# Softmax attention heads in pairs, in two row tiles and two column tiles of TensorE

## The chip, the cores and the metric

The kernel runs on one core of a Trainium2 chip. The metric is the device time of one execution in microseconds (us). The kernel before has a median of 1285.93 us over 3 runs (1284.1 to 1291.37).

## What is computed

A decoder trunk of four residual layers over 256 tokens of width 1024, batch 1. Layer 0 and layer 3 mix tokens with sliding-window attention (SWA: 16 query heads, 4 key/value heads, head width 64, window 128, rotary, a learned sink logit per head). Layer 1 is gated linear attention (GLA). Layer 2 is forgetting attention (FoX: 16 heads, no rotary, a cumulated log forget gate added to the scores). Every mixer is followed by a dense SwiGLU network (FFN). The two softmax mixers are what matters here:

```python
# swa_mixer, per block n of 128 queries, over this block's and the previous block's keys
scores = einsum('bnqkgd,bnskd->bnkgqs', qb, kk) * hd ** -0.5      # masked to the band
probs = softmax(concatenate([scores, sink_col], -1))[..., :-1]
out = einsum('bnkgqs,bnskd->bnqkgd', probs, vv) ; return out @ w_o
# fox_mixer, per block i of 128 queries, over all keys up to t1
s = einsum('bhqd,bhkd->bhqk', q, k) * hd ** -0.5 + lc[t0:t1] - lc[:t1]   # causal
o = einsum('bhqk,bhkd->bhqd', softmax(s), v) ; return o @ w_o
```

## The kernel before

Activations lie feature by token (8 tiles of 128 features by 256 tokens). Weights are float32; each piece of a weight is split by ACT (`wh`, L195) and DVE (`wl`, L197) into a high and a low part, and a product with weights is three matmuls (`mm3`, L260 to L262). Conditioning vectors (`ada`) are made on DVE (L217) or POOL (L212). A `Stream` holds the weights in order of use with five raw buffers; the SP queue issues the next load when a buffer is free.

The order of the work is written out by a Python generator. The projections call `tick()` after every two k steps; each tick emits a share of the pending weight pieces and, if a background generator runs, `bg_rate` steps of it. The background generator of the softmax layers is `attn_heads` (L529): it emits a part of the attention and yields. It is started after the first group of queries and runs beside the three other groups' projections (8 ticks each) and then beside the first half of the output projection (`out_proj`, 16 ticks), where `need_k(k)` forces as many steps as the k-th 128 features of the output need, and `bg_drain` ends it. The rates are `BG_SWA` (start rate, steps already due, rate in the output projection; first layer 0, then layer 3) and `FOX_RATE`.

`attn_heads` goes head by head in a pipeline of depth three. In iteration n it emits, up to its first `yield`: the scores of head n (L544: 128 queries by 128 keys; L545: 128 queries by 256 keys; float32, which the chip runs as two matmuls each) into one PSUM bank of tag `s` (2 buffers); the products with v of head n-2 (L551, L552) into 64 of the 128 rows of the bank `o` (1 buffer); for head n-1 the reciprocal of the row sums (DVE, L556) and the scaling of the probabilities (ACT L557 for block 0, DVE L558 for block 1); then for head n the masked minimum (DVE, L572, two instructions) and the exponentials with row sums (ACT, L577, two instructions). Up to its second `yield`: three transposes of head n-1's probabilities (PE, L585) into a bank `t` (2 buffers) and their copy to `pt` (ACT, L596); for every second head the split of `o` into `oh`, `ol` (L493, L494) that the output projection reads. That is 19 iterations of 2 steps, 38 steps.

In SWA the q and k of an even head lie in partitions 0 to 63 and those of an odd head in partitions 64 to 127, so that the matmuls L544 and L545 contract over 64 rows of the array. In FoX they contract over 66 rows from partition 0 (64 of the head and 2 for the gate). In both, a head's product with v has 64 columns of weights, and odd and even heads write to different halves of the bank `o`. The queries of SWA are transposed four heads at a time (`swa_qT`, L644), called by `pre` two heads ahead.

```python
sc = self.ps("s")
nc.tensor.matmul(sc[:, :P], q[:, :P], k[:, :P], start=True, stop=True)          # L544
nc.tensor.matmul(sc[:, P:3 * P], q[:, P:], k, start=True, stop=True)            # L545
...
nc.tensor.matmul(o[rows, :S], v[0], pt[:, :S], start=True, stop=False)          # L551
nc.tensor.matmul(o[rows, P:S], v[1], pt[:, S:], start=False, stop=True)         # L552
```

The framework that builds the program may set an engine's instructions in another order than they are written, within their dependencies; the trace shows the order in which they ran.

Of the kernel before, what the change touches and what calls it, by code (L numbers as in the profile page):

```python
# [13 lines left out]
AF = mybir.ActivationFunctionType  # L14
ALU = mybir.AluOpType
PSUM = bass.MemoryType.PSUM

P = 128
D = 1024
KT = D // P  # L20
S = 256
NB = S // P
DEPTH = 4
HD = 64
# [4 lines left out]
BIG = 1e30  # L29
# [24 lines left out]
RAW = 5  # L54
MIX_POOL = ((), (), (), ())
ORDER0 = "wshshshhwswwwgwwgggSwHSwHSSHHw"
BG_SWA = ((1.05, -6.5, 3.9), (0.544, 2.0, 1.367))
ROPE_ADD = (('gpsimd', 'gpsimd'), ('vector', 'vector'))
EARLY = 2
POOL_ADA = {(0, 0): (0, 1, 2, 4, 5), (0, 1): (7,), (0, 2): (1, 3, 4), (0, 3): (0, 1, 2, 4, 5), (0, 4): (1, 3, 4, 7)}  # L60
# [6 lines left out]
MIX_SPAN = (3, -2)  # L67
GLA_ORDER = ('z', 'r1', 'q0', 'k0', 'b', 'k1', 'q1', 'r2', 'v1', 'r3', 'v2', 'v3')
GLA_RATE = (0.585, 2.55)
FOX_RATE = (0.556, -7.0, 0.586, 0.885)  # L70
STAT = (1, 1, 1)
PSBUFS = {"mm": 3, "s": 2, "t": 2, "o": 1}

# [70 lines left out]
class Builder:  # L144
# [384 lines left out]
    def attn_heads(self, pool, heads, mask, oh, ol):  # L529


        nc = self.nc
        n_heads = len(heads)
        sms, prs, pts, rds, os_ = {}, {}, {}, {}, {}
        blocks = ((0, P, 0, P), (P, 3 * P, 129, 385))
        heads[0]["pre"]()
        for n in range(n_heads + 3):
            if n < n_heads:
                hd = heads[n]
                while not hd["ready"]():  # L540
                    yield
                q, k = hd["q"](), hd["k"]()
                sc = self.ps("s")
                nc.tensor.matmul(sc[:, :P], q[:, :P], k[:, :P], start=True, stop=True)  # L544
                nc.tensor.matmul(sc[:, P:3 * P], q[:, P:], k, start=True, stop=True)  # L545
            j = n - 2
            if 0 <= j < n_heads:
                o = os_[j // 2] = self.ps("o") if j % 2 == 0 else os_[j // 2]
                pt, v = pts.pop(j), heads[j]["v"]()
                rows = slice((j % 2) * HD, (j % 2 + 1) * HD)  # L550
                nc.tensor.matmul(o[rows, :S], v[0], pt[:, :S], start=True, stop=False)  # L551
                nc.tensor.matmul(o[rows, P:S], v[1], pt[:, S:], start=False, stop=True)  # L552
            j = n - 1
            if 0 <= j < n_heads:
                pr, rd, dn = prs[j], *rds.pop(j)
                nc.vector.reciprocal(rd, dn)  # L556
                nc.scalar.activation(pr[:, :P], pr[:, :P], AF.Copy, scale=rd[:, 0:1])  # L557
                nc.vector.tensor_scalar(out=pr[:, 129:385], in0=pr[:, 129:385],  # L558
                                        scalar1=rd[:, 1:2], scalar2=None, op0=ALU.mult)
            if n < n_heads:  # L560
                sm = self.t(pool, [P, 386], "sm", bufs=2)
                pr = prs[n] = self.t(pool, [P, 386], "pr", bufs=3)
                nm = self.t(self.small, [P, 2], "nm", bufs=3)
                dn = self.t(self.small, [P, 2], "dn", bufs=3)
                rds[n] = (self.t(self.small, [P, 2], "rd", bufs=3), dn)
                ns, e = hd["sink"], 0
                if ns is not None:
                    e = 1
                    nc.gpsimd.tensor_copy(sm[:, P:P + 1], ns)
                    nc.gpsimd.tensor_copy(sm[:, 385:386], ns)  # L570
                for b, (so, s1, po, p1) in enumerate(blocks):
                    nc.vector.tensor_tensor_reduce(  # L572
                        out=sm[:, po:p1], in0=sc[:, so:s1], in1=mask[:, so:s1], scale=1.0,
                        scalar=BIG if ns is None else ns, op0=ALU.add, op1=ALU.min,
                        accum_out=nm[:, b:b + 1])
                for b, (so, s1, po, p1) in enumerate(blocks):
                    nc.scalar.activation(pr[:, po:p1 + e], sm[:, po:p1 + e], AF.Exp, scale=-1.0,  # L577
                                         bias=nm[:, b:b + 1], accum_out=dn[:, b:b + 1])
            yield
            j = n - 1  # L580
            if 0 <= j < n_heads:
                pr = prs.pop(j)
                tp = self.ps("t")
                for i, po in enumerate((0, 129, 257)):
                    nc.tensor.transpose(tp[:, i * P:(i + 1) * P], pr[:, po:po + P], self.c("ident"))  # L585
            if n + 2 < n_heads:
                while not heads[n + 2]["pre"]():
                    yield
            if n >= 3 and n % 2:
                j = (n - 3) // 2  # L590
                self.split_hl(os_.pop(j)[:, :S], oh[:, j], ol[:, j])
                self.done_k = j + 1
            j = n - 1
            if 0 <= j < n_heads:
                pts[j] = self.t(pool, [P, 3 * P], "pt", bufs=2)
                nc.scalar.copy(pts[j], tp[:, :3 * P])  # L596
            yield


# [56 lines left out]
    def swa_heads(self, layer, pool, q_of, kT, v, oh, ol):  # L656
        nc = self.nc
        j = 0 if layer == 0 else 1
        nsink = self.t(pool, [P, 16], "nsink", bufs=1)
        nc.vector.tensor_scalar(out=nsink, in0=self.c("sinks")[:, 16 * j:16 * j + 16], scalar1=-1.0,  # L660
                                scalar2=None, op0=ALU.mult)
        qTs = {}

        def head(h):
            g, i = divmod(h, 4)
            rows = slice((i % 2) * HD, (i % 2 + 1) * HD)

            def pre():
                q = q_of(g)
                if i == 0 and q is not None:  # L670
                    qTs[g] = self.swa_qT(pool, q)
                return q is not None
            return {
                "pre": pre, "ready": lambda: True,
                "q": lambda: qTs[g][rows, i // 2],
                "k": lambda: kT[0][rows, g],
                "v": lambda: [v[:, b, g * HD:(g + 1) * HD] for b in range(NB)],
                "sink": nsink[:, h:h + 1],
            }
        return self.attn_heads(pool, [head(h) for h in range(16)], self.c("swamask"), oh, ol)  # L680
# [37 lines left out]
    def swa(self, layer, oh, ol, pool):  # L718
# [21 lines left out]
        for g in range(4):  # L740
            parts = self.proj_tok(self.st.get(f"i{layer}_{2 + g}"), hs)
            qr[g] = self.swa_q(pool, parts)
            if g == 0:
                self.bg_start(gen, *BG_SWA[layer > 0][:2])
        self.bg_rate = BG_SWA[layer > 0][2]

# [20 lines left out]
    def fox(self, layer, oh, ol, pool):  # L767
# [12 lines left out]
        for g in range(4):  # L780
            if g == 3:
                self.bg_rate = FOX_RATE[2]
            grp[g] = t = [self.t(pool, [66, 4, S], "qA", bufs=2), self.t(pool, [66, 4, S], "kA", bufs=2)]
# [39 lines left out]
            if g == 0:  # L823
                self.bg_start(gen, *FOX_RATE[:2])
        self.bg_rate = FOX_RATE[3]

# [534 lines left out]
```

## Time and profile before

| what | value |
|---|---|
| median of 3 runs | 1285.93 us |
| the profiled execution's own time | 1287.15 us |
| its span, first to last instruction | 1285.4 us |
| granted TensorE clock, mean | 0.993 |
| PE busy | 1223.3 us, 95% of the span |
| DVE busy | 1029.2 us, 80% |
| ACT busy | 719.4 us, 56% |
| attention in layer 0, layer 2, layer 3 | about 73 to 135 us, 698 to 782 us, 1012 to 1075 us |

PE is TensorE's matmuls, DVE VectorE, ACT ScalarE, POOL GpSimd. A matmul's duration holds its way through the array, so consecutive matmuls overlap in the table; what a matmul costs is read from the start of one to the start of the next. Busy shares are means over stages with different limits; a stage is read from its own stretch.

### The profile page before, as it was taken

To read this page: it belongs to the slowest core of one execution; us is meant where nothing else is said; L and a number is where in the kernel's file an instruction comes from. 1 tells how busy PE (TensorE), PEld (TensorE's weight loads), DVE (VectorE), ACT (ScalarE), POOL (GpSimd) and SP (SyncE) were. 2 spreads that over 40 slices of the span, in tenths; PEclk is the share of its full clock that TensorE was granted. 3 is DMA by queue.
4 is the path that set the end of the run, shared out by engine and by line. 5 is a ranking of instruction groups with operands and counts; after the bars stand their busy time and mean duration, and the time that the engine had idled before them with its cause. 6 is when DMAs were issued, how large, how long until landed. Compare 5 with 4: busy or idle time off the path is not lost.

```text
span 1285.4 us, 19492 instructions
## 1 busy us (share of the span) xinstructions
PE 1223.3 (95%) x7284; PEld 1061.3 (83%) x7284; DVE 1029.2 (80%) x1839; ACT 719.4 (56%) x1323; POOL 200.5 (16%) x211
## 2 busy tenths in 40 slices
PE   3698999999999999999999999999999999999997
PEld 2676888888898998888899889888889878888886
DVE  5999998878779889888877657988787977766553
ACT  4567764444576665444448766644445667644442
POOL 5468110001105321000120101100011012000011
PEclk9999999999999999999999999999999999999999
DMA  8665779977744436997875443799777434665450
GB/s 328 256 231 196 267 290 358 340 262 266 264 161 167 165 132 231 352 340 279 271 280 210 157 170 109 275 357 336 273 266 257 168 128 139 222 214 202 161 176 33
DMA packets 44673, 298.50 MB, mean 232 GB/s; under 512 B 5169, under 2 KB 5329, under 8 KB 14242
## 3 DMA queue, kind: packets, MB, share of 16 engines
q1 hardware_dynamic: 43778, 295.53, 63.7%
q8 instruction: 57, 0.93, 0.3%
q10 hardware_dynamic: 432, 1.20, 0.2%
q0 software_dynamic: 368, 0.53, 0.1%
q14 instruction: 38, 0.31, 0.1%
HBM read 296.15 MB, written 1.05 MB: 231 GB/s over the span
## 4 chain that ended last, share of the span: by engine, by line
PE 83%; DVE 9%; ACT 3%; issue 2%; DMA 2%; POOL 1%; DVEq 0%; SPq 0%; POOLq 0%; ACTq 0%
PE mm L1100 13%; PE mm L260 12%; PE mm L261 11%; PE mm L262 11%; PE mm L1102 7%; PE s L260 6%; PE s L261 6%; PE s L262 6%; DVE raw L217 2%; DVE wl L197 2%; PE o L551 2%; PE t L1071 1%; PE s L545 1%; DMA raw<-in_ada 1%; PE t L585 1%
## 5 line engine op out<-in xcount | busy, mean ns | idle before, releaser
L197 DVE TENSOR_TENSOR wl<-raw,wh 128x1024 fp32r<-128x1024 f32 (+2 forms) x408 | 454.6, 1147 | 85.5 <-ACT wh L195 84.3
L195 ACT CAST wh<-raw 128x1024 fp32r<-128x1024 f32 (+2 forms) x408 | 376.5, 963 | 224.2 <-issue 105.9
L1100 PE MATMUL mm<-a,wh 128*128 128x512 f32 x704 | 248.8, 395 | 0.0
L217 DVE CUSTOM_DVE_ANT_0 raw<-raw,cact,const 128x1024 f32<-128x1024 f32 x174 | 230.0, 1337 | 15.3 <-DMA raw<-in_ada 15.3
L260 PE MATMUL mm<-wh,hh 128*128 128x512 f32 (+1 forms) x560 | 200.5, 358 | 20.1 <-ACT hh L437 20.1
L1102 PE MATMUL mm<-a,wl 128*128 128x256 f32 x704 | 199.5, 283 | 0.0
L262 PE MATMUL mm<-wh,hl 128*128 128x512 f32 (+1 forms) x560 | 195.5, 350 | 1.3 <-DVE hl L430 1.3
L261 PE MATMUL mm<-wl,hh 128*128 128x512 f32 (+1 forms) x560 | 195.4, 349 | 0.0
L416 POOL TENSOR_TENSOR sq<-sq,sq 128x256 f32<-128x256 f32 x54 | 59.7, 1105 | 751.2 <-ACT sq L405 731.8
L1100 PEld LDWEIGHTS mm<-a,wh 128*128 128x128 f32 x704 | 132.4, 188 | 29.7
L260 PE MATMUL s<-wh,hh 128*128 128x512 f32 (+2 forms) x384 | 144.7, 378 | 2.9 <-ACT hh L437 2.9
L261 PE MATMUL s<-wl,hh 128*128 128x512 f32 (+2 forms) x384 | 143.0, 373 | 0.2 <-DVE wl L197 0.2
L262 PE MATMUL s<-wh,hl 128*128 128x512 f32 (+2 forms) x384 | 142.2, 374 | 0.0
L260 PEld LDWEIGHTS mm<-wh,hh 128*128 128x128 f32 x560 | 108.4, 194 | 36.2 <-ACT hh L437 21.0
L1102 PEld LDWEIGHTS mm<-a,wl 128*128 128x128 f32 x704 | 132.8, 189 | 0.2
L262 PEld LDWEIGHTS mm<-wh,hl 128*128 128x128 f32 x560 | 107.6, 193 | 14.9 <-DVE hl L430 2.0
L261 PEld LDWEIGHTS mm<-wl,hh 128*128 128x128 f32 x560 | 108.4, 194 | 12.5 <-issue 0.7
L497 DVE SCALAR_TENSOR_TENSOR x<-mm,mod,x 128x256 f32<-128x256 f32 x128 | 61.2, 481 | 44.5 <-PE mm L1102 35.4
L260 PEld LDWEIGHTS s<-wh,hh 128*128 128x128 f32 x384 | 72.5, 189 | 15.3 <-ACT hh L437 3.4
L261 PEld LDWEIGHTS s<-wl,hh 128*128 128x128 f32 x384 | 72.3, 188 | 12.4 <-DVE wl L197 0.5
L262 PEld LDWEIGHTS s<-wh,hl 128*128 128x128 f32 x384 | 71.7, 188 | 12.8
L260 PE MATMUL mm<-oh,wh 128*128 128x256 f32 x256 | 74.7, 297 | 2.6 <-DVE x L497 2.5
(223 smaller groups left out, 2154.6 us busy)
## 6 DMA issues: line engine op xcount, KB each, us to landing
raw<-in_ada SPq DMA_DIRECT2D x96, 1024.0 KB, 6.8
raw<-in_gu SPq DMA_DIRECT2D x88, 1024.0 KB, 6.5
raw<-in_down SPq DMA_DIRECT2D x64, 704.0 KB, 4.9
raw<-in_swa_in SPq DMA_DIRECT2D x12, 1024.0 KB, 5.1
raw<-in_gla_in SPq DMA_DIRECT2D x11, 1024.0 KB, 6.9
raw<-in_fox_in SPq DMA_DIRECT2D x11, 1024.0 KB, 5.3
raw<-in_swa_o SPq DMA_DIRECT2D x8, 1024.0 KB, 5.0
raw<-in_gla_o SPq DMA_DIRECT2D x4, 1024.0 KB, 4.8
```

The costliest lines, as they stand in the source:

```text
L195: nc.scalar.copy(wh[:, sl], raw[:, sl])
L197: eng.tensor_tensor(out=wl[:, sl], in0=raw[:, sl], in1=wh[:, sl].bitcast(F32), op=ALU.subtract)
L217: nc.vector.tensor_tensor_reduce(out=w, in0=w, in1=self.cact, scale=1.0, scalar=b, op0=ALU.mult, op1=ALU.add, accum_out=col)
L260: nc.tensor.matmul(out, ah, bh, start=first, stop=False)
L261: nc.tensor.matmul(out, ah, bl, start=False, stop=False)
L262: nc.tensor.matmul(out, al, bh, start=False, stop=last)
L416: (eng or nc.gpsimd).tensor_tensor(out=q, in0=self.acc, in1=q, op=ALU.add)
L497: self.nc.vector.scalar_tensor_tensor(out=self.x[:, m], in0=ps, scalar=gate[:, m:m + 1], in1=self.x[:, m], op0=ALU.mult, op1=ALU.add)
L545: nc.tensor.matmul(sc[:, P:3 * P], q[:, P:], k, start=True, stop=True)
L551: nc.tensor.matmul(o[rows, :S], v[0], pt[:, :S], start=True, stop=False)
L1100: nc.tensor.matmul(o, wh[:, k], a[:, kk].rearrange("p e n -> p (e n)"), start=kk == 0, stop=False)
L1102: nc.tensor.matmul(o[:, S:], wl[:, k], a[:, kk, 0], start=False, stop=kk == FT - 1)
```

## The change

Heads are taken in pairs (8 pairs, 11 iterations of 4 steps, 44 steps). The step up to the first `yield` holds the scaling of pair n-1 (one reciprocal on four columns) and then the scores of pair n: the first block of the even head, the first block of the odd head, then the second blocks in the same order, into both banks `s`; then the minima and exponentials of both heads. The second step holds the products with v of pair n-2, even and odd head in turns. The third step holds the six transposes of pair n-1 and their copies, and the `pre` of the next pair. The fourth holds the split of `o`. All rates are raised by about the ratio of the step counts.

```diff
-BG_SWA = ((1.05, -6.5, 3.9), (0.544, 2.0, 1.367))
+BG_SWA = ((1.2, -6.5, 4.5), (0.63, 2.0, 1.6))
-FOX_RATE = (0.556, -7.0, 0.586, 0.885)
+FOX_RATE = (0.64, -7.0, 0.68, 1.02)
@@ attn_heads (the loop over heads is replaced by this one over pairs)
+        for n in range(n_pairs + 3):
+            j = n - 1
+            if 0 <= j < n_pairs:
+                pr, (rd, dn) = prs[j], rds.pop(j)
+                nc.vector.reciprocal(rd, dn)
+                for e in range(2):
+                    nc.scalar.activation(pr[:, e, :P], pr[:, e, :P], AF.Copy,
+                                         scale=rd[:, 2 * e:2 * e + 1])
+                    nc.vector.tensor_scalar(out=pr[:, e, 129:385], in0=pr[:, e, 129:385],
+                                            scalar1=rd[:, 2 * e + 1:2 * e + 2], scalar2=None,
+                                            op0=ALU.mult)
+            if n < n_pairs:
+                pair = heads[2 * n:2 * n + 2]
+                for hd in pair:
+                    while not (hd["pre"]() and hd["ready"]()):
+                        yield
+                qk = [(hd["q"](), hd["k"]()) for hd in pair]
+                scs = [self.ps("s") for _ in pair]
+                for so, s1, k1 in ((0, P, P), (P, 3 * P, 2 * P)):
+                    for sc, (q, k) in zip(scs, qk):
+                        nc.tensor.matmul(sc[:, so:s1], q[:, so:so + P], k[:, :k1], start=True, stop=True)
+                pr = prs[n] = self.t(pool, [P, 2, 386], "pr", bufs=2)
...
+                for e, (hd, sc) in enumerate(zip(pair, scs)):
...
+            yield
             j = n - 2
+            if 0 <= j < n_pairs:
+                o = os_[j] = self.ps("o")
+                pt = pts.pop(j)
+                vs = [heads[2 * j + e]["v"]() for e in range(2)]
+                for b in range(2):
+                    for e in range(2):
+                        rows = slice(e * HD, (e + 1) * HD)
+                        nc.tensor.matmul(o[rows, b * P:S], vs[e][b],
+                                         pt[:, e, :S] if b == 0 else pt[:, e, S:],
+                                         start=b == 0, stop=b == 1)
             yield
             j = n - 1
+            if 0 <= j < n_pairs:
                 pr = prs.pop(j)
+                pt = pts[j] = self.t(pool, [P, 2, 3 * P], "pt", bufs=1)
+                for e in range(2):
+                    tp = self.ps("t")
+                    for i, po in enumerate((0, 129, 257)):
+                        nc.tensor.transpose(tp[:, i * P:(i + 1) * P], pr[:, e, po:po + P], self.c("ident"))
+                    nc.scalar.copy(pt[:, e], tp[:, :3 * P])
+            if n + 1 < n_pairs:
+                while not heads[2 * n + 2]["pre"]():
                     yield
+            yield
+            j = n - 2
+            if 0 <= j < n_pairs:
                 self.split_hl(os_.pop(j)[:, :S], oh[:, j], ol[:, j])
                 self.done_k = j + 1
             yield
@@ swa_heads, pre
-                if i == 0 and q is not None:
+                if g not in qTs and q is not None:
```

## Rows read from the trace of the kernel before

**Rows 1.** The page's chain that ended last: shares of the span by engine.
```profile
PE 83%; DVE 9%; ACT 3%; issue 2%; DMA 2%; POOL 1%; DVEq 0%; SPq 0%; POOLq 0%; ACTq 0%
```
**Rows 2.** Busy time in the attention stretches: layer 0, layer 2, layer 3 (two).
```profile
core 0: us, PE busy (x) PEld busy (x) DVE busy (x) ACT busy (x) POOL busy (x), PEclk, DMA share, GB/s
73.00:135.00 62.00, 57.73 (x359) 42.61 (x359) 60.25 (x153) 45.27 (x130) 44.38 (x45) 1.00 0.50 184
698.00:782.00 84.00, 83.80 (x615) 73.47 (x613) 51.63 (x141) 59.79 (x151) 5.56 (x8) 1.00 0.44 158
1012.00:1041.00 29.00, 28.95 (x191) 23.13 (x189) 24.93 (x85) 20.23 (x53) 3.04 (x14) 1.00 0.55 197
1041.00:1075.00 34.00, 34.00 (x215) 25.72 (x213) 23.91 (x75) 24.44 (x70) 3.26 (x14) 1.00 0.27 95
```
**Rows 3.** PE's timeline, layer 3, one head's blocks: start us, us, instructions.
```profile
1023.20 0.29 PE L262 MATMUL mm<-wh,hl 128*128 128x256 f32 x1
1023.42 0.48 PE L544 MATMUL s<-uh,qT 64*128 64x128 f32 x2
...
1024.27 0.39 PE L260 MATMUL mm<-wh,hh 128*128 128x256 f32 x1
1024.49 0.28 PE L261 MATMUL mm<-wl,hh 128*128 128x256 f32 x1
1024.61 0.29 PE L262 MATMUL mm<-wh,hl 128*128 128x256 f32 x1
...
1024.85 0.28 PE L261 MATMUL mm<-wl,hh 128*128 128x256 f32 x1
1025.06 0.65 PE L551 MATMUL o<-pt,v 128*64 128x256 f32 x2
...
1025.86 0.39 PE L262 MATMUL mm<-wh,hl 128*128 128x256 f32 x1
1026.08 0.28 PE L260 MATMUL mm<-wh,hh 128*128 128x256 f32 x1
```
**Rows 4.** PE's timeline, layer 0, where two heads' matmuls stand together.
```profile
119.20 0.50 PE L544 MATMUL s<-uh,qT 64*128 64x128 f32 x4
119.53 0.61 PE L545 MATMUL s<-uh,qT 64*128 64x256 f32 x4
120.07 0.39 PE L260 MATMUL mm<-oh,wh 128*128 128x256 f32 x1
...
134.69 0.66 PE L551 MATMUL o<-pt,v 128*64 128x256 f32 x4
...
135.50 0.39 PE L262 MATMUL mm<-oh,wl 128*128 128x256 f32 x1
```
**Rows 5.** PE's timeline, layer 2 (FoX), one head's blocks.
```profile
715.64 0.28 PE L262 MATMUL mm<-hh,wl 128*128 128x256 f32 x1
715.76 0.39 PE L544 MATMUL s<-kA,qA 66*128 66x128 f32 x2
...
716.51 0.65 PE L551 MATMUL o<-pt,ul 128*64 128x256 f32 x2
...
717.31 0.39 PE L260 MATMUL mm<-hh,wh 128*128 128x256 f32 x1
```
**Rows 6.** DVE's groups by line, layer 0, 73 to 135 us.
```profile
L558 DVE TENSOR_SCALAR pr<-pr,rd 128x256 f32<-128x256 f32 x16 | 17.6, 1108 | 0.0
...
L556 DVE RECIPROCAL rd<-dn 128x2 f32<-128x2 f32 x16 | 2.3, 151 | 0.2 <-ACT pr L577 0.2
```
**Rows 7.** DVE's groups by line, layer 3, 1012 to 1075 us.
```profile
L558 DVE TENSOR_SCALAR pr<-pr,rd 128x256 f32<-128x256 f32 x16 | 5.6, 351 | 0.0
...
L556 DVE RECIPROCAL rd<-dn 128x2 f32<-128x2 f32 x16 | 2.6, 161 | 2.9 <-ACT pr L577 2.8
```
**Rows 8.** ACT's groups by line, layer 3, 1012 to 1075 us.
```profile
L577 ACT ACTIVATE pr<-sm,nm 128x129 f32<-128x129 f32 (+1 forms) x32 | 14.3, 449 | 1.0 <-DVE nm L572 0.9
...
L577 ACT ACTIVATION_READ_ACCUMULATOR pr<-sm,nm 128x1 f32 x32 | 6.0, 188 | 0.0
```

More of the change, by code (lines that the diff above doesn't have):

```diff
@@ L532, in attn_heads @@
         nc = self.nc
-        n_heads = len(heads)
-        sms, prs, pts, rds, os_ = {}, {}, {}, {}, {}
+        n_pairs = len(heads) // 2
+        prs, pts, rds, os_ = {}, {}, {}, {}
         blocks = ((0, P, 0, P), (P, 3 * P, 129, 385))
         heads[0]["pre"]()
[L537 to L545, printed above, removed]
-            j = n - 2
[L547 to L578, printed above, removed]
@@ new lines, in attn_heads @@
+        for n in range(n_pairs + 3):
[20 more added lines that the diff above has]
+                pr = prs[n] = self.t(pool, [P, 2, 386], "pr", bufs=2)
+                nm = self.t(self.small, [P, 4], "nm", bufs=2)
+                dn = self.t(self.small, [P, 4], "dn", bufs=2)
+                rds[n] = (self.t(self.small, [P, 4], "rd", bufs=2), dn)
+                for e, (hd, sc) in enumerate(zip(pair, scs)):
+                    sm = self.t(pool, [P, 386], "sm", bufs=2)
+                    ns, x = hd["sink"], 0
+                    if ns is not None:
+                        x = 1
+                        nc.gpsimd.tensor_copy(sm[:, P:P + 1], ns)
+                        nc.gpsimd.tensor_copy(sm[:, 385:386], ns)
+                    for b, (so, s1, po, p1) in enumerate(blocks):
+                        nc.vector.tensor_tensor_reduce(
+                            out=sm[:, po:p1], in0=sc[:, so:s1], in1=mask[:, so:s1], scale=1.0,
+                            scalar=BIG if ns is None else ns, op0=ALU.add, op1=ALU.min,
+                            accum_out=nm[:, 2 * e + b:2 * e + b + 1])
+                    for b, (so, s1, po, p1) in enumerate(blocks):
+                        nc.scalar.activation(pr[:, e, po:p1 + x], sm[:, po:p1 + x], AF.Exp, scale=-1.0,
+                                             bias=nm[:, 2 * e + b:2 * e + b + 1],
+                                             accum_out=dn[:, 2 * e + b:2 * e + b + 1])
+            yield
+            j = n - 2
+            if 0 <= j < n_pairs:
[8 more added lines that the diff above has]
+                                         start=b == 0, stop=b == 1)
@@ L579, in attn_heads @@
             yield
             j = n - 1
-            if 0 <= j < n_heads:
+            if 0 <= j < n_pairs:
                 pr = prs.pop(j)
[L583 to L587, printed above, removed]
+                pt = pts[j] = self.t(pool, [P, 2, 3 * P], "pt", bufs=1)
[4 more added lines that the diff above has]
+                    nc.scalar.copy(pt[:, e], tp[:, :3 * P])
@@ L588, in attn_heads @@
+            if n + 1 < n_pairs:
+                while not heads[2 * n + 2]["pre"]():
                     yield
-            if n >= 3 and n % 2:
-                j = (n - 3) // 2
+            yield
+            j = n - 2
+            if 0 <= j < n_pairs:
                 self.split_hl(os_.pop(j)[:, :S], oh[:, j], ol[:, j])
                 self.done_k = j + 1
[L593 to L596, printed above, removed]
```

## Prediction

> **What bounds the kernel now.** I read the chain that ended last first: 83% of it is PE, 9% DVE and 3% ACT [rows 1]. So PE time taken away should come off the end, as long as PE is the engine that ends last in the stages touched. Then I cut the stages out by windows, because the change touches three stretches only, 209 of the span's microseconds [rows 2]. In layer 2 (FoX) PE is busy 83.8 of 84 us while DVE has 51.6 and ACT 59.8: PE alone sets the pace. In layer 3 PE is busy throughout too (28.95 of 29, 34 of 34), but DVE stands close behind in the first part (24.9 of 29) and DVE and ACT have 23.9 and 24.4 of 34 in the second. In layer 0 the order is reversed: DVE is busy 60.25 of 62 us, PE 57.7. The reader is to see that one and the same saving on PE meets three different limits.
>
> The third view is PE's own timeline, start to start. Beside a head's block the projection's matmuls follow one another every 0.12 us (1024.49 to 1024.61) [rows 3]. The scores of one SWA head last from 1023.42 to 1024.27, 0.85 us. The step into the block is 0.22 and the first step after it 0.22, each 0.10 over the regular one, so a head's scores cost PE 0.85 + 0.20 = 1.05 us. The products with v go from 1025.06 to 1025.86, 0.80, with 0.09 going in and 0.10 coming out: 0.99 us [rows 3].
>
> **What a pair costs.** The trace of before has it already. The order on PE is not quite the written one, and in layer 0 the scores of two neighbouring heads happen to stand together at 119.20: eight matmuls instead of four, and the next matmul starts at 120.07, after 0.87 us. The same happened once to the products with v: eight of them from 134.69 to 135.50, 0.81 us [rows 4]. Two heads take 0.01 to 0.02 us more than one: the two halves of the array work at the same time. So:
>
> - A pair of SWA scores: 2 x 1.05 before, 0.87 + 0.20 after, 1.03 saved.
> - A pair of products with v, SWA and FoX: 2 x 0.99 before, 0.81 + 0.19 after, 0.98 saved. FoX's block is the same length, 716.51 to 717.31 [rows 5].
> - A pair of FoX scores: nothing. They use 66 rows of the array, which is more than one half, and the step from the projection into them is the regular 0.12 (715.64 to 715.76) [rows 5]: the array is not divided for them, so taking them in turns overlaps nothing.
>
> On PE that is 8 x (1.03 + 0.98) = 16.1 us in layer 3, 16.1 - 2.0 = 14.1 in layer 0 where one pair of each kind is together already [rows 4], and 8 x 0.98 = 7.8 in FoX. The sum, 38 us, is the upper bound; the lower is nothing. The stages decide.
>
> **FoX, 7 us of 7.8.** PE at 83.8 - 7.8 = 76.0 stays far above ACT's 59.8 and DVE's 51.6 [rows 2]. What ends last stays PE. I leave 0.8 for the last pair, whose exponentials, scaling, transposes and products now come as two heads' worth with only the output projection's ticks beside them. Bounds 4 to 7.8.
>
> **Layer 3, 9 us of 16.1.** In 1012 to 1041 PE would fall by 16.1 x 29/63 = 7.4 to 21.6. DVE has 24.9; one reciprocal per pair in place of two (0.16 each, rows of two columns; I take the four-column one alike) gives back 4 x 0.16 = 0.6 [rows 2, 7]. DVE then sets the stretch at 24.3 and the gain is at most 4.7; I take 4. In 1041 to 1075 PE falls by 8.7 to 25.3, beside ACT's 24.4 and DVE's 23.3 [rows 2]. At most 8.7 is gained, but only if three engines whose work hangs on one another all stay busy. I take 5, for two reasons. `need_k(3)` now wants 24 steps where 0.63 x 24 + 2 = 17.1 are done when the output projection begins (before: 20, with 0.544 x 24 + 2 = 15.1 done), so that 7 steps instead of 5 are emitted with little projection between. And the transposed queries of the last group are now made two steps ahead of their scores instead of four, in just those forced steps. Bounds 4 to 13.4.
>
> **Layer 0, 2 us of 14.1.** DVE's idle time is 62 - 60.25 = 1.75 us [rows 2], and the reciprocals give 8 x 0.15 = 1.2 [rows 6]. That would be 3; I take 2, as the steps come densest here (4.5 a tick after the projections). The bounds are wide: of DVE's busy time, the scaling L558 takes 1108 ns a piece against 351 in layer 3 [rows 6, 7]; those 16 x 0.76 = 12 us are waiting while POOL is busy 44.4 of the 62 us, and a new order can make it shorter or longer. Bounds -3 to 8.
>
> **What costs nothing, and why.** ACT's and POOL's instructions keep their number and shape. The two `s` banks now belong to one pair, so the next scores wait for the minima of the last pair; four steps lie between, some six ticks of 6 x 0.12 = 0.72 us in layer 3. Without that cover each pair would wait for about its minima. `pt` has one buffer, but the products that read it are written one step ahead of the transposes that refill it. `o` is filled in one step and read two later, before the next fill. No transfer moves in the program. The SP queue's loads follow the ticks; the DMA share is 0.27 to 0.55 [rows 2], so a stage shortened by a sixth still finds its weights.
>
> **Sum.** 2 + 7 + 9 = 18 us. The profiled execution took 1287.15, so 1269.2; it was 1.2 over the median 1285.93, so against the runs shown the forecast is **1268 us**, 1.4% faster. Half a percent, 6.4 us, is about what a measurement of this kernel can tell from no change.
>
> **Rivals.**
>
> 1. PE's saving comes through whole in layers 2 and 3 (DVE is not a limit at 24.9 of 29, since part of its busy time is spent in waits) and partly in layer 0: 14 + 7.8 + 6 = 28, **1258**. For it: layer 3's PE is busy without a gap. Against: DVE's 24.9 of 29 and 60.25 of 62 [rows 2]. Chance 0.12.
> 2. DVE and ACT, which empty the score and transpose banks, set the pace of both SWA layers, so that only FoX's 7 and 2 us of the second part of layer 3 are left: 9, **1277**. For it: DVE's 60.25 of 62 and 24.9 of 29 [rows 2]. Against: the 9.6 us by which ACT stands under PE in 1041 to 1075 [rows 2]. The Trainium skill has this as a rule ("TensorEngine Tiling (Array Packing)", Performance Considerations, PSUM Bottleneck): tiling speeds up TensorE but not the emptying of PSUM, which can become the limit. By that rule the time would be this rival's. Chance 0.14.
> 3. The change does not do what it says: the program as built sets the matmuls of a pair apart, as it set matmuls of different steps together at 119.20 [rows 4]. What is left is a few switches of the array fewer: 2 us, **1284**. Against: each pair's eight matmuls are written in one piece, and become ready together once both banks are free. Chance 0.08.
> 4. Slower. The reciprocal stands first in the step and at the head of DVE's queue, and behind it wait the `wl` pieces that the projection needs. It waits for the last exponential of a pair, 4 x (0.45 + 0.19) = 2.6 us of ACT instead of 1.3 [rows 8]. Before, it waited 2.9 us over 16 in layer 3 [rows 7]. If each of the 24 reciprocals waits 1.3 us more, 31 us go and 18 come: +13, **1299**. It decides from 18/24 = 0.75 us per pair. Against: in the projection stretches four steps lie between the exponentials and the reciprocal. Chance 0.06.
>
> **The numbers.** My forecast has 0.60, with a range of its own of 1262 to 1276. The range for 8 in 10 reaches into rival 1 and past rival 2: 1255 to 1281; it leaves out some of rival 1 and rivals 3 and 4. Faster than 1279.5 are the forecast, rival 1 and most of rival 2: 0.83. Rival 3 and the rest of rival 2 are within half a percent: 0.11. Slower: 0.06.
>
> **What would show it.** In the profile after, on PE's timeline, L544's and L545's successors stand as eight matmuls from one start to the next stranger in about 0.87 us in layers 0 and 3, and the products with v in 0.81 in all three. FoX's scores still take some 1.3 us for a pair. The stretch of layer 2 shortens by about 7, layer 3's by about 9 with DVE near full in its first part, layer 0's by about 2 with DVE as full as before. All other stages keep their length. The prediction is wrong if PE shows new waits for the reciprocal or the scaling (rival 4), if the eight do not stand together (rival 3), or if layer 0 moves by more than 8 us, since the waits beside POOL are what I can least foresee.

## The result, and the profile after

The changed kernel took **1269.32 us** (median of 4 runs, 1267.95 to 1269.98) beside 1287.16 for the kernel before (4 runs): a ratio of 0.9856, 95% interval 0.9833 to 0.9879, so 1.4% faster. The forecast was 1268. The total is right; its parts are less so, and the experiments are mostly about those.

The chain that ended last, by engine, of the kernel after: PE's share fell from 83% to 80% and DVE's rose from 9% to 11% [rows 1].

```profile
PE 80%; DVE 11%; ACT 3%; issue 3%; POOL 1%; DMA 1%; DVEq 0%; SPq 0%; POOLq 0%; ACTq 0%
```

The attention stretches of the kernel after, as busy time of each engine (layer 0, layer 2, and layer 3 in two parts; compare [rows 2]):

```profile
core 0: us, PE busy (x) PEld busy (x) DVE busy (x) ACT busy (x) POOL busy (x), PEclk, DMA share, GB/s
73.00:135.00 62.00, 47.99 (x305) 36.94 (x306) 58.53 (x136) 40.78 (x122) 40.29 (x45) 0.83 0.45 157
699.00:777.00 78.00, 78.00 (x634) 73.59 (x633) 52.03 (x136) 57.95 (x153) 5.66 (x8) 1.00 0.51 180
1005.00:1031.00 26.00, 25.62 (x202) 21.23 (x199) 24.51 (x85) 21.13 (x59) 4.28 (x16) 1.00 0.59 210
1031.00:1054.00 23.00, 22.05 (x172) 17.07 (x170) 19.57 (x64) 18.87 (x61) 3.45 (x12) 1.00 0.34 121
```

FoX is still PE's alone (78 of 78). In layer 3 PE now has small gaps, and DVE is almost full in the first part (24.51 of 26). Layer 0 is the surprise: PE is busy for 48.0 of 62 us where it was 57.7, and its granted clock, given as a share of the higher of its two levels (1.2 and 2.4 GHz), has a mean of 0.83 where it was 1.00.

PE's timeline in layer 3 of the kernel after (start us, us, instructions of one kind in a row), around one pair's scores and one pair's products with v:

```profile
1020.00 0.28 PE L262 MATMUL mm<-wh,hl 128*128 128x256 f32 x1
1020.20 0.93 PE L559 MATMUL s<-uh,qT 64*128 64x128 f32 x8
1021.06 0.38 PE L260 MATMUL mm<-wh,hh 128*128 128x256 f32 x1
1021.28 0.28 PE L261 MATMUL mm<-wl,hh 128*128 128x256 f32 x1
...
1022.36 0.28 PE L261 MATMUL mm<-wl,hh 128*128 128x256 f32 x1
1022.56 0.87 PE L589 MATMUL o<-pt,v 128*64 128x256 f32 x8
1023.37 0.39 PE L262 MATMUL mm<-wh,hl 128*128 128x256 f32 x1
1023.59 0.28 PE L260 MATMUL mm<-wh,hh 128*128 128x256 f32 x1
```

Two heads' scores go from 1020.20 to 1021.06, 0.86 us, where one head took 0.85 [rows 3]; two heads' products from 1022.56 to 1023.37, 0.81, where one took 0.80. The steps in and out are as before (0.20 and 0.22). Not every pair looks like this. The products stand as blocks of eight everywhere, but two of the eight in layer 3 take 1.71 and 1.17 us. Of the eight pairs of scores in layer 3, six stand as blocks of eight; one has its heads apart (1007.18 and 1008.34, 0.85 each) and one is cut in two (1038.67 and 1039.51). In layer 0 seven do, and two of these take 1.5 us, each beside a wait for the minima that empty a score bank (0.8 us together). And one pair of layer 3 had stood together before the change already; the next stranger started at 1012.10, after 0.86 us:

```profile
1011.24 0.50 PE L544 MATMUL s<-uh,qT 64*128 64x128 f32 x4
1011.57 0.61 PE L545 MATMUL s<-uh,qT 64*128 64x256 f32 x4
```

The same view of FoX, after:

```profile
713.36 0.28 PE L262 MATMUL mm<-hh,wl 128*128 128x256 f32 x1
713.48 1.47 PE L559 MATMUL s<-kA,qA 66*128 66x128 f32 x8
714.61 0.47 PE L260 MATMUL mm<-hh,wh 128*128 128x256 f32 x1
...
715.38 0.28 PE L262 MATMUL mm<-hh,wl 128*128 128x256 f32 x1
715.59 0.87 PE L589 MATMUL o<-pt,ul 128*64 128x256 f32 x8
716.39 0.39 PE L260 MATMUL mm<-hh,wh 128*128 128x256 f32 x1
```

Here the products of a pair take 0.80, while its scores on 66 rows take 1.13 between starts and 0.18 more in the step behind (0.30 instead of 0.12), 1.31 together, with no switch step going in (0.12): nothing overlaps there.

To see where the time went, cut the run at marks that every version has: the first matmul of each next norm's row sums (L309). The first column is the mark itself, the others are differences of neighbouring marks, the last the mark in the final norm (there the last matmul of L320); all in us, from one profiled execution each.

| kernel | layer 0 | FFN | GLA | FFN | FoX | FFN | layer 3 | FFN | end |
|---|---|---|---|---|---|---|---|---|---|
| before | 154.9 | 189.4 | 135.8 | 189.7 | 128.3 | 188.5 | 99.7 | 191.8 | 1278.1 |
| after | 159.7 | 191.2 | 133.5 | 187.6 | 120.0 | 187.7 | 89.1 | 189.7 | 1258.5 |
| after, again (e2) | 159.8 | 190.9 | 134.6 | 187.7 | 120.0 | 187.7 | 89.2 | 189.8 | 1259.5 |
| by head (e3) | 155.7 | 192.2 | 135.2 | 187.6 | 120.0 | 187.7 | 89.4 | 189.7 | 1257.6 |
| scaling on ACT (e4) | 159.6 | 189.0 | 135.0 | 187.6 | 120.0 | 188.8 | 89.2 | 189.7 | 1258.9 |
| layer 0 single (e5) | 157.0 | 188.9 | 135.7 | 191.6 | 119.9 | 188.8 | 89.2 | 190.7 | 1261.8 |
| scores in one half (e6) | 157.1 | 191.3 | 133.6 | 187.6 | 120.0 | 187.8 | 92.3 | 189.8 | 1259.4 |
| products apart (e7) | 158.7 | 187.8 | 134.4 | 187.6 | 128.3 | 188.6 | 94.5 | 189.8 | 1269.8 |
| after, padded (e8) | 156.8 | 192.8 | 134.3 | 189.0 | 120.2 | 188.6 | 89.2 | 190.3 | 1261.1 |
| layer 0 single, aligned (e9) | 154.5 | 188.7 | 135.6 | 187.9 | 120.0 | 187.7 | 89.1 | 189.8 | 1253.3 |
| before, shifted (e10) | 155.9 | 187.7 | 135.1 | 187.6 | 128.2 | 187.9 | 99.5 | 191.2 | 1273.1 |
| layer 0 without attention (e11) | 145.6 | 189.5 | 135.4 | 188.2 | 120.0 | 187.7 | 89.2 | 189.7 | 1245.3 |
| layer 0 at the old rates (e12) | 154.3 | 191.7 | 135.0 | 187.6 | 120.0 | 188.0 | 89.1 | 189.8 | 1255.5 |

From before to after: FoX -8.3, layer 3 -10.6, and layer 0 **+4.8** with +1.8 in the FFN behind it. The remaining -7.3 lies in stages without a pair in them. So three questions stand: does the gain come from taking the heads in turns, what did layer 0 lose, and what shortened stages that the change doesn't touch?

### The profile page after: what moved, and what is told of

Same layout as the page of the kernel before. It is cut to its first block, busy times and chain, and to the rows that moved or that the text cites. A ratio compares the mean times of both kernels' runs of the same rounds, so it can differ in the third digit from the quotient of the medians.

```text
span 1266.2 us, 19497 instructions
## 1 busy us (share of the span) xinstructions
PE 1192.6 (94%) x7284; PEld 1046.0 (83%) x7284; DVE 1029.8 (81%) x1815; ACT 713.5 (56%) x1321; POOL 199.8 (16%) x211
## 4 chain that ended last, share of the span: by engine, by line
PE 80%; DVE 11%; ACT 3%; issue 3%; POOL 1%; DMA 1%; DVEq 0%; SPq 0%; POOLq 0%; ACTq 0%
PE mm L1113 12%; PE mm L260 11%; PE mm L261 11%; PE mm L262 11%; PE s L261 7%; PE s L260 7%; PE s L262 7%; PE mm L1115 7%; DVE wl L197 3%; DVE raw L217 2%; PE s L559 2%; PE t L1084 1%; PE o L589 1%; DVE pr L547 1%; ACT wh L195 1%
## 5 line engine op out<-in xcount | busy, mean ns | idle before, releaser
L1113 PE MATMUL mm<-a,wh 128*128 128x512 f32 x704 | 245.9, 392 | 0.0
L261 PEld LDWEIGHTS s<-wl,hh 128*128 128x128 f32 x384 | 72.7, 189 | 12.5 <-DVE wl L197 0.5
```

The source lines that it names most:

```text
L261: nc.tensor.matmul(out, ah, bl, start=False, stop=False)
L1113: nc.tensor.matmul(o, wh[:, k], a[:, kk].rearrange("p e n -> p (e n)"), start=kk == 0, stop=False)
```

## The experiments

**Controls.** The kernel before, once more, gives the scatter of the stages.

> The kernel before, unchanged, once more, for a second profile of its stages. In the first pair of profiles layer 0's mixer (up to the row sums of the next norm, 154.9 against 159.7 us) is 4.8 us longer after the change, layer 2's 8.2 shorter, layer 3's 10.5 shorter, and the stages that the change doesn't touch differ by -2.3 to +1.8 us. If layer 0's loss is real, the mark stands within 1 us of 154.9 again. If it is only the difference between two executions, it stands anywhere from 153 to 160, and the untouched stages move as much.

It took 1288.82; its stages are those of before within 1.0 us (155.9, 189.0, 136.0, 189.9, 128.3, 189.2, 99.7, 191.8). The kernel after, beside e6 to e8:

> The kernel after, unchanged, as the control of the three others and for a second profile of layer 0. If pairs cost layer 0 some 4 us, its mixer ends at 158 to 161 us again (159.7 in the first profile); if that was one execution's, at 155 to 157. Time 1268 to 1270.

1270.87 (1268.95 to 1272.32), ratio 0.9872 (0.9855 to 0.9889).

**Is it the turns?** e3 writes the same matmuls head after head:

```
-for so, s1, k1 in ((0, P, P), (P, 3 * P, 2 * P)):
-    for sc, (q, k) in zip(scs, qk):
+for sc, (q, k) in zip(scs, qk):
+    for so, s1, k1 in ((0, P, P), (P, 3 * P, 2 * P)):
...
-for b in range(2):
-    for e in range(2):
+for e in range(2):
+    for b in range(2):
```

> The kernel after, with the scores of a pair written head by head and the products with v too, so that a head's matmuls stand one after another in one half of the array; pairs, steps and rates stay. Theory (the gain is the two halves working at once): only the last matmul of the first head and the first of the second can still overlap, so a pair of scores takes some 1.28 us instead of 0.86 and a pair of products 1.23 instead of 0.80; FoX's stretch gets 8 x 0.43 = 3.4 us longer, layer 3's 4 to 7, layer 0's 0 to 2, and the time is 1278 (1275 to 1282). Rival (the gain is the new order of the steps and fewer changes between array modes): nothing of that changes, and the time stays at 1267 to 1271.

1267.47 (1265.35 to 1269.54), ratio 0.9836 (0.9809 to 0.9862). My theory fell: nothing was lost, and FoX and layer 3 are as after (120.0 and 89.4). PE's timeline of e3, one pair of scores in layer 3:

```profile
1018.93 0.28 PE L262 MATMUL mm<-wh,hl 128*128 128x256 f32 x1
1019.14 0.93 PE L559 MATMUL s<-uh,qT 64*128 64x128 f32 x8
1020.00 0.38 PE L260 MATMUL mm<-wh,hh 128*128 128x256 f32 x1
```

The pair still takes 0.86. Why shows in the groups of PE by line with each shape apart, cut to 1019.18 to 1019.40 in the same run:

```profile
L559 PE MATMUL s<-uh,qT 64*128 64x128 f32 x4 | 0.5, 322 | 0.0
```

A head has two matmul records with 128 columns [rows 3]; four ran by 1019.40, and none with 256. So the second head's first matmuls began ahead of the first head's second ones, which are written before them. That e3's order did reach the chip shows in FoX, where the scores don't divide the array. There a pair starts at 705.21, and until 705.75 PE has run these of it:

```profile
L559 PE MATMUL s<-kA,qA 66*128 66x256 f32 x2 | 0.6, 380 | 0.0
L559 PE MATMUL s<-kA,qA 66*128 66x128 f32 x2 | 0.4, 272 | 0.0
```

That is one head whole and none of the other, while in the kernel after the same stretch of a pair holds all four records of 128 columns and one of 256. So in SWA the two halves of the array take their matmuls on their own. The Trainium skill ("TensorE: Matmul & The Clock Gate", Part 3) says that matmuls start and end strictly in the order of the program; by these records they don't when they sit in different halves.

**Is it the halves?** e6 takes the SWA heads of each group of four in the order 0, 2, 1, 3 (and lays out the rows of the output weight to match), so that the two heads of a pair have their scores on the same 64 rows. The products are still in two halves.

```
-[head(h) for h in range(16)]
+[head(4 * (h // 4) + (0, 2, 1, 3)[h % 4]) for h in range(16)]
```

> The kernel after, with the SWA heads of each group of four taken in the order 0, 2, 1, 3 (the rows of the output weights are laid out to match), so that the q and k of the two heads of a pair lie in the same 64 partitions; everything else stays, FoX too. After the run with the matmuls written head by head, in which eight matmuls still took 0.86 us, the theory reads: what counts is that the two heads stand side by side and lie in different halves, not that they are written in turns. Then a pair of scores takes 1.3 to 1.6 us here, eight pairs cost PE 4 to 6 us in layer 3, layer 3's mixer gets 3 to 5 us longer and the time is 1273 (1270 to 1277). Rival (the halves don't matter; the gain is the block as such, with fewer changes of the array's mode): 0.9 us, and the time stays within 1 us of the control.

1270.59 (1268.88 to 1272.87), ratio 0.9867 (0.9847 to 0.9887). PE's timeline of e6:

```profile
1019.03 0.28 PE L262 MATMUL mm<-wh,hl 128*128 128x256 f32 x1
1019.24 1.57 PE L559 MATMUL s<-uh,qT 64*128 64x128 f32 x8
1020.74 0.39 PE L260 MATMUL mm<-wh,hh 128*128 128x256 f32 x1
```

1.50 us in place of 0.86: in one half the heads follow one another. Layer 3 is 3.1 longer (92.3). The whole time is that of the control, where 1273 was expected, because in the profiled execution layer 0 is 2.7 shorter; why is not shown.

**The products alone.** e7 sets the odd head's products between the transposes of two heads, with `pt` as one tile per head:

```
+for e in range(2):
+    if e and 0 <= n - 2 < n_pairs:
+        products(1)
...
```

> The kernel after, with the products with v of the odd head moved out of the second step to between the transposes of the two heads in the third step, so that the products of a pair never stand side by side; the scores stay as they are. Theory (each pair of products saved 0.98 us by standing side by side): FoX's mixer goes from 120.0 back to 126 to 128 us, layer 3's from 89.1 to 93 to 97, layer 0 stays within 3, and the time is 1280 (1276 to 1284). Rival (FoX's 8 us come from the order of the steps): FoX's mixer stays at 120 to 122, and the time at 1268 to 1272.

1279.96 (1276.92 to 1282.35), ratio 0.9938 (0.9917 to 0.9959). PE's timeline of e7 in FoX:

```profile
714.44 0.49 PE L604 MATMUL t<-const,pr 128*128 128x128 f32 x3
714.86 0.86 PE L542 MATMUL o<-pt,ul 128*64 128x256 f32 x4
715.65 0.55 PE L604 MATMUL t<-const,pr 128*128 128x128 f32 x3
```

One head's products now take 0.79 by themselves, and FoX is back at 128.3: all of FoX's gain is the products standing together. In layer 3 this gives back 5.3 (94.5), with 10 of the 16 heads apart and three pairs still together. With e6's 3.1 for the scores, both halves of the change are seen to work there; the remaining 2.2 of layer 3's 10.6 no run takes apart.

**Layer 0.** What PE waits for in 73 to 140 us of the kernel after (us in total, times, the longest):

```profile
PE t L600 <- DVE pr L547: 9.7, 7, 3.3
PE t L600 <- ACT pr L545: 2.8, 2, 1.5
```

The transposes wait 12.5 us for a pair's scaling. PE's timeline of one of these waits:

```profile
98.07 0.33 PE L600 MATMUL t<-const,pr 128*128 128x128 f32 x1
101.66 0.90 PE L600 MATMUL t<-const,pr 128*128 128x128 f32 x3 [3.26 <-DVE pr L547]
104.01 0.69 PE L600 MATMUL t<-const,pr 128*128 128x128 f32 x2 [1.45 <-DVE pr L547]
104.36 0.56 PE L262 MATMUL mm<-wh,hl 128*128 128x256 f32 x1
104.72 0.41 PE L260 MATMUL mm<-wh,hh 128*128 128x256 f32 x1
104.93 0.41 PE L261 MATMUL mm<-wl,hh 128*128 128x256 f32 x1
105.14 0.41 PE L262 MATMUL mm<-wh,hl 128*128 128x256 f32 x1
```

DVE's and then POOL's timeline there:

```profile
95.91 3.35 DVE L217 CUSTOM_DVE_ANT_0 raw<-raw,cact,const 128x1024 f32<-128x1024 f32 x1
99.19 0.08 DVE L217 DVE_READ_ACCUMULATOR2_ANT mod<- 128x1 f32 x1
99.19 4.77 DVE L547 TENSOR_SCALAR pr<-pr,rd 128x256 f32<-128x256 f32 x2
```

```profile
95.80 8.01 POOL L212 TENSOR_TENSOR raw<-raw,cact 128x1024 f32<-128x1024 f32 x3
```

While POOL works, two scalings take 4.77 us on DVE (2.4 each; 0.35 in layer 3, [rows 7]), PE stands behind them in order, and afterwards its 256-column matmuls follow every 0.21 us instead of 0.12: the granted clock has fallen to the lower level. From 84 to 132 us its mean is 0.81 after. The Trainium skill ("SBUF — State Buffer", Terms, shared port pair) has VectorE and GpSimd exclude one another on a pair of ports for a whole instruction; the 2.4 beside 0.35 agrees with that.

e4 takes layer 0's larger scaling off DVE:

```
-nc.vector.tensor_scalar(out=pr[:, e, 129:385], in0=pr[:, e, 129:385], ...)
+nc.scalar.activation(pr[:, e, 129:385], pr[:, e, 129:385], AF.Copy,
+                     scale=rd[:, 2 * e + 1:2 * e + 2])
```

> The kernel after, with the scaling of block 1 of layer 0 on ACT instead of DVE; nothing else. Theory (layer 0 lost because the two scalings of a pair stand on DVE behind POOL's conditioning products, PE's transposes stand behind them, and PE's idle time then lowers the granted clock): PE's 12.5 us of waits for the scaling go down to under 4, the granted clock of 96 to 132 us comes back to 0.95 or more, layer 0's mixer ends at 149 to 155 us instead of 159.7, and the time is 1261 (1258 to 1265). Rival (layer 0 is set by DVE's amount of work, which hardly changes when waits are taken away, or by the denser steps): 1267 to 1271.

1266.7 (1265.8 to 1268.32), ratio 0.9828 (0.9799 to 0.9856). The theory fell as written. The waits move rather than go away, as e4's view of PE's waits shows (72 to 140 us):

```profile
PE s L563 <- DVE nm L576: 2.6, 1, 2.6
PE t L604 <- ACT pr L545: 2.1, 3, 1.3
```

So does the low clock: it is 0.96 from 96 to 132 us, as the theory said (after: 0.75), but 0.69 from 132 to 154. Layer 0 keeps its 159.6 and the FFN behind it comes to 189.0; the two together give back 2.3 of 6.6. DVE beside POOL is not the whole cause.

e5 keeps pairs in layers 2 and 3 and puts the old loop and its old rates back in layer 0:

```
+run = self.attn_heads if layer else self.attn_heads_single
-return self.attn_heads(pool, [head(h) for h in range(16)], ...)
+return run(pool, [head(h) for h in range(16)], ...)
```

> The kernel after, with layer 0 done head by head with the loop and the rates of the kernel before; layers 2 and 3 in pairs. Theory (pairs cost layer 0 4.8 us and gave the rest in layers 2 and 3): layer 0's mixer ends at 154 to 156 us and the time is 1264.5 (1262 to 1267). Rival (the difference of layer 0 is one between executions): 1268 to 1271.

1267.85 (1265.68 to 1270.9), ratio 0.9841 (0.9811 to 0.987). Layer 0 and its FFN come to 345.9 (after: 350.9), yet the next FFN lengthens by 4.0 to 191.6, with nothing in it changed. That led to the tensors' place, below. e11 asks what attention is worth at all in layer 0: it leaves out that layer's scores, softmax and products.

```
+if self.layer == 0:
+    for j in range(n_pairs):
+        for _ in range(4):
+            yield
+        self.split_hl(self.x[:, j], oh[:, j], ol[:, j])
+        self.done_k = j + 1
+    return
```

> The kernel after without the scores, softmax and products of layer 0 (its steps emit only the splits that the output projection reads, of the residual in place of the attention's output). Theory (layer 0's mixer is set by the stream of weights and conditioning, which DVE, POOL and the loads work off, so that attention's time on PE can't show there): the mixer still ends at 145 us or later, against 154.9 before and 159.7 after. Rival (layer 0 is set by the attention): it ends some 25 us earlier, at 130 to 137 us.

1254.71 in one run, and its waits of PE between 60 and 165 us begin so:

```profile
PE mm L260 <- ACT wh L195: 20.3, 1, 20.3
PE mm L260 <- DVE mod L215: 7.4, 1, 7.4
```

Even with no attention the mark stands at 145.6, only 9.3 before that of before: PE waits 20.3 us for a weight's split and 7.4 for the conditioning's products. So at most 9.3 of the 154.9 us before hung on the attention with all its engines. The rest is paced by the weights and the conditioning going through ACT, DVE and POOL, and PE time saved there has little to show in.

e12 is the kernel after with one number pair changed, the rates at which layer 0's attention steps are issued:

```
-BG_SWA = ((1.2, -6.5, 4.5), (0.63, 2.0, 1.6))
+BG_SWA = ((1.05, -6.5, 3.9), (0.63, 2.0, 1.6))
```

> The kernel after, with layer 0's attention issued at the rates it had before (1.05 steps a tick during the projections and 3.9 after them, in place of 1.2 and 4.5); layers 2 and 3 keep theirs. Theory: what layer 0 loses lies in the pair itself (two scalings in a row on DVE beside POOL's products, and PE standing behind them), not in how densely the steps come. Then the first mark stays at 157 to 160 us, layer 0 with its FFN at 347 to 351, and the time within 3 us of the kernel after, 1266 to 1273. Rival: the denser steps leave PE too little projection between a pair's exponentials, its scaling and its transposes. Then PE's waits for the scaling, 12.5 us, fall to under 6, layer 0 with its FFN comes to 343 to 346 as with single heads, and the time to 1263 to 1266.

1264.62 (1262.78 to 1264.96), ratio 0.98 (0.9769 to 0.9831). The rival was mostly right. PE's waits in 73 to 140 us of e12:

```profile
PE t L600 <- DVE pr L547: 4.8, 4, 1.8
PE s L559 <- DVE nm L572: 3.1, 3, 1.5
PE o L589 <- DVE ol L494: 2.0, 2, 1.6
```

The wait for the scaling by DVE halves and that by ACT is gone, though a scaling takes no less than after (1285 ns in the mean beside 1229), and the mark stands at 154.3, as before. What is lost is in the FFN behind it, 191.7 against 188.7 in e9, where PE waits for the FFN's input in e12 (155 to 346 us):

```profile
PE s L260 <- ACT hh L437: 2.4, 1, 2.4
```

The same wait is 3.1 us in the kernel after and in e2, e3, e6 and e8, whose FFN takes 190.9 to 192.8, and 1.5 in e4 (189.0). There is none in before, e1, e5, e7, e9 and e10, whose FFN takes 187.7 to 189.4. So what the FFN behind layer 0 loses goes with this wait. In the kernel after ACT's copy of the norm's row scales (`rbs`, L467) starts 1.36 us after their matmul, and DVE's next step (`tk`, L435) 1.1 us after that copy; in e9 these are 0.65 and 0.04. The difference is 1.8 us: each of the two engines splits two weights first there (1.98 us on ACT, 2.36 on DVE). Why these splits stand there is open.

**The tensors' place.** The pair version keeps its score statistics `nm`, `dn` and `rd` in two buffers each instead of three, and everything laid out behind that pool of small tiles moves by 96 bytes; the weights `wh` and `wl` are laid out ahead of it and stay. The FFN's activation tile `a` begins at byte 179,296 of a partition before, 179,200 after, and 179,488 in e5. e8 takes the shift back with an unused tile:

```
+pad = self.t(self.small, [P, 24], "pad", bufs=1)
+nc.vector.memset(pad[:, :1], 0.0)
```

> The kernel after, with 96 bytes more in the pool of small tiles (a tile that is not used) and one small memset at the start, so that what is allocated behind that pool, the FFN's activations among it, lies where it lay before the change. In the first profiles the FFN of layers 1 and 3 is 2.1 us shorter after the change, and its matmuls of 256 columns follow one another after 117.6 in place of 118.9 ns, though no line of it was touched. Theory (the smaller score tiles moved these tensors by 96 bytes): the spacing and the FFN stages go back to those of before, 189.7 and 191.8 us, and the time is 1273 (1271 to 1276). Rival (another cause, or the difference of two executions): the stages stay at 187.6 and 189.7 and the time within 1 us of the control.

1273.17 (1270.56 to 1274.3), ratio 0.9884 (0.9866 to 0.9901): 2.3 us over the control and the way that was expected, but the two intervals overlap, and of the FFNs of layers 1 and 3 only part comes back (189.0 and 190.3). e10 gives the kernel before the shift alone, by two buffers instead of three for the three tiles:

```
-nm = self.t(self.small, [P, 2], "nm", bufs=3)
+nm = self.t(self.small, [P, 2], "nm", bufs=2)
...
```

> The kernel before with two buffers in place of three for the three smallest score tiles (row minima, row sums, reciprocals): the order of the instructions on PE is the same, and all that is allocated behind the pool of small tiles lies 96 bytes lower, as in the kernel after. Theory (part of the gain is the place of the FFN's activations): the spacing of the 256-column matmuls of the FFN goes from 118.9 to 117.6 ns, the FFN of layers 1 and 3 to 187.6 and 189.7 us, and the time is 1283 (1281 to 1285) against 1287 of before. Rival: 1286 to 1288.

1283.88 (12 runs, 1281.7 to 1286.74), ratio 0.9969 (0.9956 to 0.9981): 4.0 us with no pair in it. The layers with attention keep their length (155.9, 128.2, 99.5), so the missing buffers cost nothing that shows; the FFN of layer 1 comes to the expected 187.6, that of layer 3 only to 191.2 (189.7 was expected). The group of the FFN's matmuls on `a` (500 to 660 us; the last number before the second bar is the mean in ns), first before, then e8, then after, then e10:

```profile
L1100 PE MATMUL mm<-a,wh 128*128 128x512 f32 x153 | 54.0, 395 | 0.0
```

```profile
L1113 PE MATMUL mm<-a,wh 128*128 128x512 f32 x144 | 50.8, 395 | 0.0
```

```profile
L1113 PE MATMUL mm<-a,wh 128*128 128x512 f32 x146 | 50.9, 391 | 0.0
```

```profile
L1100 PE MATMUL mm<-a,wh 128*128 128x512 f32 x162 | 56.5, 391 | 0.0
```

In the mean the matmul that reads `a` takes 395 ns at one place and 391 at the other, whichever loop the attention has. e9 is e5 with 224 bytes of padding, which puts `a` at 179,712, a multiple of 512 as 179,200 is:

```
+pad = self.t(self.small, [P, 56], "pad", bufs=1)
+nc.vector.memset(pad[:, :1], 0.0)
```

> The kernel with layer 0 head by head and layers 2 and 3 in pairs, as run before, with 224 bytes more in the pool of small tiles (a tile that is not used) and one small memset at the start: the FFN's activations then lie at a multiple of 512 bytes, as in the kernel after, and not 288 bytes past one. Theory (pairs cost layer 0 and its FFN 4 to 5 us; the first run of this version lost them again to the place of the activations, with 191.6 us for the FFN of layer 1): FFN of layer 1 at 187.6 us, layer 0 and its FFN at 345 to 347 us, time 1264 (1261 to 1267), 5 us under the control. Rival (neither is real): 1267 to 1271.

**1262.44** (5 runs, 1262.16 to 1264.9), ratio 0.9808 (0.979 to 0.9827): the FFN is back at 187.9 and this is the lowest median of the versions that compute everything. Its layer 0, from 84 to 132 us:

```profile
84.00:132.00 48.00, 44.41 (x271) 32.11 (x272) 46.63 (x119) 34.42 (x102) 34.46 (x37) 1.00 0.46 166
```

PE is busy for 44.4 of 48 us and keeps the full clock. e12, with pairs everywhere and layer 0 at the old rates, can't be told from e9, whose interval lies inside its own.

## Why the prediction was right, step by step

- **A pair of SWA scores, and of products: right where the pair stands together.** Predicted 0.87 and 0.81, measured 0.86 and 0.81 or 0.80, with the switches as forecast. In layer 3 this holds for six of the eight pairs of scores and six of the products. FoX's scores: no overlap, as forecast. The short stretch in the trace of before where two heads happened to meet [rows 4] carried the forecast.
- **The reason "in turns" was never tested by it.** I read [rows 4] as two heads standing together, and that is what counts (e3), in different halves (e6).
- **FoX, 7: measured 8.3**, just over its upper bound of 7.8; e7 ties all of it to the products. What the last half microsecond is stays open.
- **Layer 3, 9: measured 10.6**, inside 4 to 13.4. On PE, 4.8 came off the score blocks (12.9 to 8.1) and 5.0 off the products' (12.7 to 7.7); and 16 blocks fewer (18 instead of 34) to switch into and out of, 0.19 each, make 3.0. That is 13, not the 16.1 of the forecast. Two pairs of scores and two of products fell short, and one pair had not been to gain in the first place, since it stood together in the kernel before (1011.24); the forecast took such a pair off in layer 0 alone. The stretch from the first scores on fell from 63.3 to 48.8 us, but 3.8 of that is given back behind it, where more of the output projection is left. DVE is near full in the first part, as forecast.
- **Layer 0, -2: measured +4.8, and +1.8 in its FFN.** This step failed; its lower bound was a loss of 3. I wrote that the steps come densest here and took off 1 us for it. The density is what cost: at the old rates (e12) the time is 1264.62 in place of 1269.32, with intervals of the ratios that just miss each other, and the mark stands at 154.3, lower than in every version at the dense rates (155.7 to 159.8). Layer 0 and its FFN together take 346.0 there; at the dense rates they scatter from 346.5 to 350.9, and with single heads they take 343.2 (e9) to 345.9 (e5). Of the 2.8 us between e12 and e9, the wait for the FFN's input is 2.4. It is not separated how much of the loss is PE standing behind the scaling and how much the clock that falls after it; the clock alone it is not, since e12 has a mean of 0.86 from 84 to 132 us and no loss at the mark. From 73 to 154 us the three profiles with the latest mark (after, e2 and e4, 159.6 to 159.8) do have the lowest mean, 0.85 to 0.87; before, e1, e9 and e10 have 0.98 and marks of 154.5 to 155.9; but e7, with 0.94 and 158.7, and e12, with 0.92 and 154.3, break the order. So the clock goes with the loss and is not shown to be its cause. That pairs gain nothing here is shown by e12 beside e9 (154.3 and 154.5 at the mark), and e11 bounds what there was to gain: without any attention the mark comes only 9.3 us earlier.
- **All other stages keep their length: wrong.** They gave 7.3. About 4 of it is the tensors' new place (e10 against before). The rest is within what these stages scatter by (GLA, say, 133.5 to 136.0) and not settled.
- **The sum** of 18 came out (17.8 between the medians) by luck: layer 0's 8.6 too many were met by 2.9 more from FoX and layer 3 and by 7.3 from stages that I had left out.
- **The rivals.** 1 (1258) is what PE's whole saving would give; only e9 and e12 come nearer to it, by not losing in layer 0. 2, the engines that empty the banks, does not hold where the gain is: layer 3 got 10.6, not 2. In layer 0 PE does wait for DVE and ACT, but 12.5 us of it end at the scaling, which works on `pr` and empties no bank, and 0.8 at the minima, which do. So the Trainium skill's rule ("TensorEngine Tiling (Array Packing)", Performance Considerations, PSUM Bottleneck) did not decide here. 3 is refuted: 8 of 8 pairs of products stand as blocks of eight in all three layers, and of the SWA scores 13 of 16. 4 is refuted in its mechanism: none of PE's waits in these stretches ends at the reciprocal, and DVE's idle time before it fell from 7.2 us to 3.1 over the whole run. Its neighbour came instead, the scaling behind it: PE waited for DVE's scaling for 2.7 us in layer 0 before, and for scalings on both engines for 12.5 after. New waits for the scaling were one of the prediction's own signs of being wrong, and for layer 0 it was.

## What to carry to other kernels

Two small matmuls that use different halves of the array run at once if they merely stand side by side and neither has to wait; look in the old trace for a place where that has happened by chance, and price the change by it. Before counting the saving, ask stage by stage which engine sets the end, and retune the rate at which work is issued for each of these stages separately: the denser rates cost layer 0 some 5 us, while layers 2 and 3 gained with theirs. When stages that a change doesn't touch move by one per cent, compare where the tensors lie, and repeat the old kernel with that shift alone.

## What the hardware showed that I had not expected

- Matmuls in different halves of the array start out of their written order (e3: four records of 128 columns by 1019.40, none of 256), while FoX's, written by the same lines, keep it.
- Where an operand lies changes a matmul's time: 395 ns against 391 in the mean for the same 512-column matmul with `a` 96 bytes apart; the shift was worth some 4 us in 1287 (e10). Both quick places are multiples of 512 bytes; which rule decides was not tried further.
- In layer 0, PE's waits of 1.5 to 3.3 us in the kernel after went together with a mean granted clock of 0.81 from 84 to 132 us; in e9, where the longest wait was 1.0, it was 1.00. In e5, with the same loop in layer 0 and waits no longer than e9's, it was 0.93, so the length of the waits alone does not decide.
